# A chunk's output products grouped by form with the inverse's and the state's products, and low-rank second passes over all 128 weight rows

## The chip, the cores and the metric

The kernel runs on one core of a Trainium2 chip. The metric is the device time of one execution in microseconds (us). Three timed runs of the kernel before took 1186.85, 1188.13 and 1191.43 us; the median is 1188.13. One further execution was recorded by the hardware profiler.

The engines are named as in the profile: PE is the matmul engine, PEld its weight loads, DVE the vector engine, ACT the scalar engine, POOL the general one, SP the engine that issues most DMAs.

## What is computed

One layer of a hybrid block on 512 tokens of width 1024: an RMS norm, one wide input projection, three token mixers side by side (a gated short convolution, a gated linear recurrence, an RWKV-7 time mixing), a gated sum, an output projection, and an MLP with a squared ReLU. The part at issue is the RWKV-7 recurrence with 16 heads of 64 channels. Token by token the reference has:

```python
def step(state, inp):
    r_t, w_t, k_t, v_t, kk_t, a_t = inp
    sa = jnp.einsum('bhvk,bhk->bhv', state, -kk_t)
    state = (state * w_t[:, :, None, :]
             + sa[..., None] * (kk_t * a_t)[:, :, None, :]
             + v_t[..., None] * k_t[:, :, None, :])
    y_t = jnp.einsum('bhvk,bhk->bhv', state, r_t)
    return state, y_t
```

The decay `w` and the factor `a` come from low-rank products, `tanh(xw) @ w2` and `xa @ a2`, whose inner dimension is 64.

## The kernel before, in words

Activations lie with channels on the 128 partitions and the 512 tokens along the free dimension. The big projections are computed in three passes of a rounded number and its remainder (`mm3`, L153 to L155): high weights by high data, high by low, low by high. Each pass is a 128x512 matmul with 128 weight rows and 128 weight columns. Weights stream from DRAM in halves of 128x512; ACT rounds each (L131, `whi`) and DVE takes the remainder (L94, `wlo`).

The 16 heads go through the recurrence in four groups of four. For each group there are:

- `krv`: keys, receptances, values and the low-rank products for the group. A low-rank product is two passes: L402 and L408 with the rounded weights over all 128 rows, L403 and L409 with the weights' remainder. The data tiles `lws` and `las` hold the rounded inputs on one half of the rows and their remainders on the other; the weights `swh` and `swl` hold the same 64 rows twice.
- `amat` and `inverse`: the matrices of each chunk of 64 tokens, and the inverse of its triangular part.
- `chain`: the walk over the eight chunks, which carries the state. Each chunk has, for the four heads e = 2h + jj:
  - L550, into `pu`: products of `AXt` (128 weight rows, 64 columns) with `sv`, which holds the state on its upper half and the values on its lower;
  - ACT copies the result to `u0` (L552, L553);
  - L558, into `pu`: the inverse `TT` (64 rows, 64 columns) by `u0`; DVE copies the result into `sv` (L559, L560);
  - L567, into `pS`: `BKT` (128 rows, 64 columns) by `sv`; DVE makes the next state of it (`Stm`, `St`), and DVE and ACT copy that into the next chunk's `sv` (L545, L546);
  - the output `py`: for each head first L582, `RT` (64 rows, 64 columns) by the state, then L584, `AXt` (128 rows, 64 columns) by `sv`, which adds to it. ACT copies `py` to `Y` (L586).
- `post`: the norm of the outputs and the gate.

These products are float32, and each is two records in the profile. A group's first chunk starts from zero and leaves L582 out; the last chunk leaves L567 out. `pu`, `pS` and `py` have one buffer each, a PSUM bank.

A critical generator (`amat`, `inverse`, `chain`, `post`) is woven with a filler that issues projections of the same or the next group (`weave`, `segments`): after every step of the critical part some steps of the filler are emitted, by shares that are given as numbers. The critical part has a higher priority. The framework's scheduler then orders the instructions of each engine by priority and by its own estimates of when operands are ready; each engine executes its own list in order. `pin` (L157) is an exception: a matmul passed to it with a true first argument keeps its place behind the matmuls that the program emitted before it.

Of the kernel before, what the change touches and what calls it, by code (L numbers as in the profile page):

```python
# [9 lines left out]
F32 = mybir.dt.float32  # L10
# [8 lines left out]
P = 128  # L19
# priorities of the weight stream, the prologue and the critical steps over what is emitted beside them  # L20
OFF, OFFS, OFFP = 160, 20, 30
CP, CPI, CPP = 150, 60, 30
# empty steps that leave the latency of an inverse, or of a norm, to the filler
NINV, NPOST = 16, 6
# steps of the fillers, and their shares by part of the critical path
N_AB, N_KRV = 28, 24
# [3 lines left out]
S = 512  # L30
# [3 lines left out]
NC = 8  # L34
L = 64
# [53 lines left out]
def block_kernel(ctx, tc, xt, win, par, mulr, sw, wout, w1, w2, fg, cst, eyes, out):  # L89
    nc = tc.nc  # L90
    v, ac, gp, pe, sy = nc.vector, nc.scalar, nc.gpsimd, nc.tensor, nc.sync
# [18 lines left out]

# [1 line left out]
    ident = cp.tile([P, P], F32, name="ident")  # L112
    bd = cp.tile([P, P], F32R, name="bd")
    mask = cp.tile([P, P], F32, name="mask")
    part = cp.tile([P, len(PAR), KT], F32, name="part")
# [5 lines left out]

# [1 line left out]
    def load_w(src):  # L123
# [33 lines left out]
    def pin(first, mm):  # L157
        # in the order of the program, behind the matmuls before it
        if first:
            tc.keep_in_program_order(mm)  # L160

    def rsqrt(x, y, t):
        # Newton's steps from a first guess on the exponent; within 2 ulp after the third
        ts2(y.bitcast(I32), x.bitcast(I32), -0.5, RSQ, MUL, ADD)
        for _ in range(3):
            tt(t, x, y, MUL)
            stt(t, t, -0.5, y, MUL, MUL)
            stt(y, t, 1.5, y, ADD, MUL)

    def rsqrt_rows(pool, o, ps, low, scale=1.0):  # L170
        # rows alike in each 32: tokens to partitions, the root there, and back
        w = pool.tile([P, S], F32, tag="rqw", name="rqw")
        q = pool.tile([P, 3, 16], F32, tag="rqq", name="rqq")
        v.transpose(w, ps)
        wv = w.rearrange("p (b j) -> p b j", j=32)[:, :, 0]
        if scale == 1.0:
            v.tensor_scalar(out=q[:, 0], in0=wv, scalar1=low, scalar2=None, op0=MAX)
        else:
            ts2(q[:, 0], wv, scale, low, MUL, ADD)
        rsqrt(q[:, 0], q[:, 1], q[:, 2])  # L180
        v.transpose(o, q[:, 1].unsqueeze(2).to_broadcast([P, 16, 32]))

    # =======================================================================
    # projections and the three branches
    # =======================================================================
    ht_ctx = ExitStack()
# [7 lines left out]
    pc = ps.enter_context(tc.tile_pool(name="pc", bufs=1, space=PSUM))  # L194
# [99 lines left out]

    # low-rank inputs, and the first key tile, on x before its norm's scale
    def unscaled(t, tag):
# [8 lines left out]

    # derived per-channel values
    # sigmoid(z) = (1 + tanh(z / 2)) / 2 throughout: tanh shares its table with exp
    for i, (n, c) in enumerate((("mu_k", -1.0), ("mu_r", -1.0), ("ka", -0.5), ("mu_v", -1.0))):
# [12 lines left out]
    lws = sp.tile([P, S], F32R, name="lws")  # L321
    las = sp.tile([P, S], F32R, name="las")
# [14 lines left out]

    # softplus of the recurrence's parameter
    apv = part[:, PI["ap"]]
# [32 lines left out]
    def krv(g, G_):  # L372
# [5 lines left out]
        for jj in range(2):  # L378
            j = 2 * g + jj
# [3 lines left out]
            else:  # L383
                ks = WP("ks")
                t = yield from proj(("k", j))
# [11 lines left out]
            t = yield from proj(("r", j))  # L397
            shift(t, pv("mu_r", j), dvp(OMR, j), rs)
            yield
            swh, swl = load_sw(pk, "swa", j, 0, 2)  # L400
            pw = pm.tile([P, S], F32, tag="pm", name="pw")
            pe.matmul(pw, swh[:, 0], lws, start=True, stop=False)  # L402
            pe.matmul(pw, swl[0:64, 0], lws[0:64], start=False, stop=True)  # L403
            sig = WP("a1")
# [3 lines left out]
            pe.matmul(pa, swh[:, 1], las, start=True, stop=False)  # L408
            pe.matmul(pa, swl[64:128, 1], las[64:128], start=False, stop=True)  # L409
            av = WP("a4")  # L410
# [18 lines left out]
            tt(G_.BK[:, jj, :, 1], c3(kp), c3(pinv), MUL)  # L429
            # by head: the two tiles' halves side by side  # L430
            if jj == 0:
# [16 lines left out]
    def amat(G_):  # L448
        # A^T = [b|k]^T [a|r], masked
        G_.AX = sp.tile([P, 4, NC, 2, L], F32, tag="AXt", name="AXt")  # L450
# [24 lines left out]
    def inverse(G_):  # L475
# [8 lines left out]
        gp.dma_start(xt.rearrange("l s t -> l (s t)"), eyes)  # L484
        # xt[l, s, t] = X[t, s];  X[t, :] += A[t, s] X[s, :], la[l, s, t] = A[t, s]
        yield
# [39 lines left out]
    def chain(G_, c_lo, c_hi):  # L526
# [4 lines left out]
        St = G_.St  # L531
        for c in range(c_lo, c_hi):
# [22 lines left out]
            for jj in range(2):  # L555
                for h in range(2):
                    e = 2 * h + jj
                    pe.matmul(pu[64 * h:64 * h + 64, 2 + jj], TT[:, e * 8 + c], u0[:, e], start=True, stop=True)  # L558
            v.tensor_copy(sv[0:64, 0:2], pu[0:64, 2:4])  # L559
            v.tensor_copy(sv[0:64, 2:4], pu[64:128, 2:4])  # L560
            yield
            Sn = None
            if c < NC - 1:
# [9 lines left out]
                else:  # L573
                    tm = sp.tile([P, 2, L], F32, tag="Stm", name="Stm", bufs=2)
                    tt(tm, pS, St, ADD)
                    tt(Sn, tm, pl, MUL)
            py = pc.tile([P, S], F32, tag="py", name="py")[:, 0:2 * L].rearrange("p (j v) -> p j v", j=2)
            for jj in range(2):
                for h in range(2):
                    o = py[64 * h:64 * h + 64, jj]  # L580
                    if St is not None:
                        pe.matmul(o, RT[64 * h:64 * h + 64, jj, c], St[64 * h:64 * h + 64, jj],  # L582
                                  start=True, stop=False)
                    pe.matmul(o, AXt[:, 2 * h + jj, c, 1], sv[:, 2 * h + jj],  # L584
                              start=St is None, stop=True)
            ac.copy(G_.Y[:, c], py)  # L586
# [54 lines left out]
    def ab(q):  # L641
        # the recurrent branch, then the convolution's
        px = W("u2")
# [134 lines left out]
    for g in range(NG - 1):  # L778
        fl = fill_main(g)
        # steps of the two fillers, spread over 31 + 24 + 10 steps of the critical part  # L780
        nab = 2 * N_AB - (21 * R0 if g == 0 else 0)
        r2 = ((1 - P1) * nab + N_KRV) / (24 + 10 * WPOST)
        segments([(chainit(amat(GS[g]), inverse(GS[g])), P1 * nab / 31), (chain(GS[g], 0, NC), r2),
                  (post(g, GS[g]), WPOST * r2)], fl)
        drain(fl)

# [1 line left out]
    G_ = GS[NG - 1]  # L788
# [96 lines left out]

    # =======================================================================
    # MLP; the second norm's scale goes to its end
    # =======================================================================
    NA = 3 * NF // 4
    with tc.tile_pool(name="mw", bufs=2) as mw, \  # L890
# [34 lines left out]
        gp.memset(epst, EPS)  # L925
        # the square of the second norm's scale, by token
        sc2 = cp.tile([P, 4], F32, name="sc2")
# [127 lines left out]
```

## Time and profile before

| | us |
|---|---|
| timed runs, median of 3 (lowest, highest) | 1188.13 (1186.85, 1191.43) |
| profiled execution, span from first to last instruction | 1188.4 |
| PE busy | 1155.3 |
| DVE busy | 786.9 |
| ACT busy | 550.5 |
| the four walks over the chunks, first to last product | 55.2, 52.6, 52.6, 70.0 |

The profiler gives the profiled execution's span, with no time around it; it lies 0.3 us above the median of the timed runs. The walks are the stretches 180.5 to 235.7, 366.8 to 419.4, 550.6 to 603.2 and 716.6 to 786.6 us of the span. The last is longer because its filler and the norm of the first half of its tokens lie in it.

A row of the timeline has the start, the duration, the engine, the line, the operation, what it writes and reads, and the form. For PE the form is weight rows*weight columns, then rows x columns of the moving data. Matmuls overlap in the pipeline, so the cost of one on PE is read from start to start.

### The profile page before, as it was taken

What the parts mean: (1) busy time and instruction counts of PE and PEld (TensorE: products, weight loads), DVE (VectorE), ACT (ScalarE), POOL (GpSimd) and SP (SyncE); (2) the same over time, 40 slices, a digit from 0 to 9 for tenths busy, and PEclk for the clock granted to TensorE, in tenths of its full rate; (3) what the DMA queues carried; (4) which work ended last, traced back from release to release, by engine and by line L of the source; (5) the groups of instructions that cost most, each with busy time, mean ns of one, the idle gap of its engine ahead of it and who ended that gap; (6) DMA issues with size and microseconds to landing.
All of it is one profiled execution on the core that took longest, in us unless ns stands there. A gap on an engine that the chain in (4) does not pass through costs nothing.

```text
span 1188.4 us, 17270 instructions
## 1 busy us (share of the span) xinstructions
PE 1155.3 (97%) x6396; PEld 896.6 (75%) x6396; DVE 786.9 (66%) x1537; ACT 550.5 (46%) x1005; POOL 59.2 (5%) x99
## 2 busy tenths in 40 slices
PE   8999989999999999989999989999999999999996
PEld 4677876677777677767677766889888888888885
DVE  7997985689975678985688975677544444222225
ACT  6655364444556443565444545556444443222224
POOL 4100000000000000000000011000000000000003
PEclk9899988999999999999999999999999999999999
DMA  5231230222332122233122244436323333433322
GB/s 183 89 89 54 89 98 28 63 85 71 96 114 72 41 80 80 85 106 90 46 80 67 71 126 150 151 116 187 124 90 98 89 98 118 154 101 91 105 89 98
DMA packets 61973, 114.69 MB, mean 97 GB/s; under 512 B 7232, under 2 KB 10816, under 8 KB 61888
## 3 DMA queue, kind: packets, MB, share of 16 engines
q1 hardware_dynamic: 54960, 95.49, 26.2%
q0 software_dynamic: 6352, 17.30, 4.6%
q8 instruction: 50, 0.82, 0.3%
q10 hardware_dynamic: 576, 0.79, 0.2%
q14 instruction: 35, 0.29, 0.1%
HBM read 104.64 MB, written 8.91 MB: 96 GB/s over the span
## 4 chain that ended last, share of the span: by engine, by line
PE 84%; DVE 12%; issue 2%; ACT 1%; DMA 0%; SPq 0%; DVEq 0%; ACTq 0%
PE pp L153 12%; PE pp L155 11%; PE pp L154 11%; PE acc L153 6%; PE acc L154 6%; PE acc L155 6%; PE p L155 5%; PE p L153 5%; PE p L154 5%; DVE wlo L94 3%; PE py L582 2%; PE pA L458 2%; PE py L584 2%; DVE Z L94 2%; DVE dg L94 2%
## 5 line engine op out<-in xcount | busy, mean ns | idle before, releaser
L94 DVE TENSOR_TENSOR wlo<-raw,whi 128x512 fp32r<-128x512 f32 x340 | 235.4, 695 | 250.6 <-ACT whi L131 241.7
L131 ACT CAST whi<-raw 128x512 fp32r<-128x512 f32 x340 | 209.7, 619 | 379.1 <-PE acc L155 124.5
L155 PE MATMUL pp<-hh,wlo 128*128 128x512 f32 x696 | 284.4, 410 | 14.8 <-DVE wlo L94 14.5
L153 PE MATMUL pp<-hh,whi 128*128 128x512 f32 x696 | 285.0, 412 | 1.3 <-ACT hh L254 1.3
L154 PE MATMUL pp<-hl,whi 128*128 128x512 f32 x696 | 282.1, 407 | 3.1 <-DVE hl L97 3.1
L155 PEld LDWEIGHTS pp<-hh,wlo 128*128 128x128 f32 x696 | 133.2, 191 | 53.1 <-DVE wlo L94 21.6
L153 PEld LDWEIGHTS pp<-hh,whi 128*128 128x128 f32 x696 | 133.2, 191 | 34.6 <-issue 1.9
L154 PEld LDWEIGHTS pp<-hl,whi 128*128 128x128 f32 x696 | 133.4, 192 | 33.6 <-DVE hl L97 3.7
L155 PE MATMUL p<-h2h,wlo 128*128 128x512 f32 (+1 forms) x264 | 103.0, 390 | 0.1
L153 PE MATMUL p<-h2h,whi 128*128 128x512 f32 (+1 forms) x264 | 103.0, 390 | 0.0
L154 PE MATMUL p<-h2l,whi 128*128 128x512 f32 (+1 forms) x264 | 102.8, 389 | 0.0
L154 PE MATMUL acc<-wlo,ah 128*128 128x512 f32 x256 | 99.7, 390 | 0.0
L155 PE MATMUL acc<-whi,al 128*128 128x512 f32 x256 | 99.6, 389 | 0.0
L153 PE MATMUL acc<-whi,ah 128*128 128x512 f32 x256 | 99.6, 389 | 0.0
L155 PEld LDWEIGHTS p<-h2h,wlo 128*128 128x128 f32 x264 | 49.7, 188 | 11.6 <-DVE wlo L94 0.3
L154 PEld LDWEIGHTS p<-h2l,whi 128*128 128x128 f32 x264 | 49.7, 188 | 11.3
L153 PEld LDWEIGHTS p<-h2h,whi 128*128 128x128 f32 x264 | 49.7, 188 | 11.3
L154 PEld LDWEIGHTS acc<-wlo,ah 128*128 128x128 f32 x256 | 48.1, 188 | 10.1 <-DVE wlo L94 0.3
L153 PEld LDWEIGHTS acc<-whi,ah 128*128 128x128 f32 x256 | 48.1, 188 | 10.1
L155 PEld LDWEIGHTS acc<-whi,al 128*128 128x128 f32 x256 | 48.1, 188 | 10.0
L94 DVE TENSOR_TENSOR Z<-Z,dg 64x31 f32<-64x31 f32 (+15 forms) x124 | 42.2, 340 | 4.1
L94 DVE TENSOR_TENSOR dg<-Z 64x31 f32<-64x31 f32 (+15 forms) x124 | 42.2, 340 | 4.1
(299 smaller groups left out, 1591.3 us busy)
## 6 DMA issues: line engine op xcount, KB each, us to landing
raw<-in_win SPq DMA_DIRECT2D x180, 256.0 KB, 2.6
raw<-in_w SPq DMA_DIRECT2D x128, 256.0 KB, 2.7
raw<-in_wout SPq DMA_DIRECT2D x32, 256.0 KB, 2.6
swr<-in_sw SPq DMA_DIRECT2D x16, 128.0 KB, 2.1
x2T<-in_xt POOLq DMA_DIRECT2D x4, 512.0 KB, 7.1
x2d<-st POOLq DMA_DIRECT2D x8, 256.0 KB, 2.8
xr<-x2d POOLq DMA_DIRECT2D x1, 2048.0 KB, 8.7
xT<-in_xt SPq DMA_DIRECT2D x3, 512.0 KB, 6.8
```

The lines of the kernel that those rows point to most:

```text
L94: return v.tensor_tensor(out=o, in0=a, in1=b, op=op)
L131: ac.copy(hi, raw)
L153: pe.matmul(ps, wh, xh, start=start, stop=False)
L154: pe.matmul(ps, wh, xl, start=False, stop=False)
L155: pe.matmul(ps, wl, xh, start=False, stop=stop)
L458: pe.matmul(pts[h][:, ci], G_.BK[rows, jj, c], G_.AR[rows, jj, c], start=True, stop=True)
L582: pe.matmul(o, RT[64 * h:64 * h + 64, jj, c], St[64 * h:64 * h + 64, jj], start=True, stop=False)
L584: pe.matmul(o, AXt[:, 2 * h + jj, c, 1], sv[:, 2 * h + jj], start=St is None, stop=True)
```

## The change

It has two parts, and comments are dropped. In `chain`, `py` is taken from its pool before the second step's end, the four products of `RT` with the state (L582 before) are emitted right behind the four products of the inverse (L558), and the four of `AXt` with `sv` (L584 before) right behind the four of the state (L567 before). Both go through a new helper, `out_mm`, and so have one line, L564. The helper pins them: the `RT` products always, the `AXt` products behind the first always and the first too except in the last chunk. Only the first product of each half of the partitions clears the bank's flags (`start`). In `krv` the second low-rank passes take all 128 rows, which adds the product of the weights' remainder with the inputs' remainder.

```diff
-            pe.matmul(pw, swl[0:64, 0], lws[0:64], start=False, stop=True)
+            pe.matmul(pw, swl[:, 0], lws, start=False, stop=True)
...
-            pe.matmul(pa, swl[64:128, 1], las[64:128], start=False, stop=True)
+            pe.matmul(pa, swl[:, 1], las, start=False, stop=True)
...
                     pe.matmul(pu[64 * h:64 * h + 64, 2 + jj], TT[:, e * 8 + c], u0[:, e], start=True, stop=True)
+            py = pc.tile([P, S], F32, tag="py", name="py")[:, 0:2 * L].rearrange("p (j v) -> p j v", j=2)
+
+            def out_mm(w, x, h, jj, first, last, behind):
+                mm = pe.matmul(py[64 * h:64 * h + 64, jj], w, x, start=first and jj == 0, stop=last,
+                               skip_group_check=True)
+                pin(behind or h + jj > 0, mm)
+
+            if St is not None:
+                for jj in range(2):
+                    for h in range(2):
+                        out_mm(RT[64 * h:64 * h + 64, jj, c], St[64 * h:64 * h + 64, jj], h, jj, True, False, True)
             v.tensor_copy(sv[0:64, 0:2], pu[0:64, 2:4])
             v.tensor_copy(sv[0:64, 2:4], pu[64:128, 2:4])
             yield
...
-            py = pc.tile([P, S], F32, tag="py", name="py")[:, 0:2 * L].rearrange("p (j v) -> p j v", j=2)
             for jj in range(2):
                 for h in range(2):
-                    o = py[64 * h:64 * h + 64, jj]
-                    if St is not None:
-                        pe.matmul(o, RT[64 * h:64 * h + 64, jj, c], St[64 * h:64 * h + 64, jj],
-                                  start=True, stop=False)
-                    pe.matmul(o, AXt[:, 2 * h + jj, c, 1], sv[:, 2 * h + jj],
-                              start=St is None, stop=True)
+                    out_mm(AXt[:, 2 * h + jj, c, 1], sv[:, 2 * h + jj], h, jj, St is None, True, c < NC - 1)
             ac.copy(G_.Y[:, c], py)
```

PE's list in the second chunk of the second group, before, from the inverse's products to the next chunk's first ones (`pp` is a projection of the filler; sizes are those of what is written):

```order
L558 MATMUL pu<-u_3399,Z 64x64 x4
L153 MATMUL pp<-hh,whi 128x512
L154 MATMUL pp<-hl,whi 128x512
L155 MATMUL pp<-hh,wlo 128x512
L567 MATMUL pS<-sv,BKT 64x64 x4
L584 MATMUL py<-sv,AXt 64x64
L582 MATMUL py<-St,RT 64x64
L584 MATMUL py<-sv,AXt 64x64
L582 MATMUL py<-St,RT 64x64
L584 MATMUL py<-sv,AXt 64x64
L582 MATMUL py<-St,RT 64x64
L584 MATMUL py<-sv,AXt 64x64
```

Behind these come three `pp`, the fourth L582 (it is the next chunk's first) and the next L550. The same place in PE's list after the change:

```order
L558 MATMUL pu<-u_3399,Z 64x64 x4
L564 MATMUL py<-St,RT 64x64 x4
L154 MATMUL pp<-hl,whi 128x512
L580 MATMUL pS<-sv,BKT 64x64
L155 MATMUL pp<-hh,wlo 128x512
L580 MATMUL pS<-sv,BKT 64x64 x3
L564 MATMUL py<-sv,AXt 64x64 x4
L153 MATMUL pp<-hh,whi 128x512
L154 MATMUL pp<-hl,whi 128x512
L155 MATMUL pp<-hh,wlo 128x512
L153 MATMUL pp<-hh,whi 128x512
L550 MATMUL pu<-sv,AXt 64x64 x4
```

The four products of `RT` moved up behind the inverse's, those of `AXt` follow the state's without a break, and one `pp` parts the first state product from its three fellows. Over the program such a cut stands at 28 places.

DVE's list in the seventh chunk of the same group, before, from the copies of the inverse's products to the copy of the state into `sv` (`rqq`, `rs` and the tiles named a belong to the filler's `krv`):

```order
L559 COPY sv<-pu 64x128
L560 COPY sv<-pu 64x128
L97 SCALAR_TENSOR_TENSOR rqq<-rqq 128x16 x2
L94 TENSOR_TENSOR wlo<-raw,whi 128x512
L94 TENSOR_TENSOR Stm<-pS,St 128x128
L94 TENSOR_TENSOR rqq<-rqq 128x16
L97 SCALAR_TENSOR_TENSOR rs<-pp,part,rs 128x511
L94 TENSOR_TENSOR St<-Stm,pl 128x128
L97 SCALAR_TENSOR_TENSOR rqq<-rqq 128x16
L406 TENSOR_SCALAR a_3830<-a_3830 128x512
L545 COPY sv<-St 64x128
```

And after:

```order
L572 COPY sv<-pu 64x128
L573 COPY sv<-pu 64x128
L94 TENSOR_TENSOR rqq<-rqq 128x16
L97 SCALAR_TENSOR_TENSOR rs<-pp,part,rs 128x511
L94 TENSOR_TENSOR Stm<-pS,St 128x128
L97 SCALAR_TENSOR_TENSOR rqq<-rqq 128x16
L406 TENSOR_SCALAR a_3830<-a_3830 128x512
L94 TENSOR_TENSOR St<-Stm,pl 128x128
L97 SCALAR_TENSOR_TENSOR rqq<-rqq 128x16
L413 SCALAR_TENSOR_TENSOR a_3838<-smk,a_3830 128x512
L545 COPY sv<-St 64x128
```

The filler's scan over the tokens (L413) moved ahead of the state's copy, and a `wlo` moved ahead of the copies L572 and L573. On SP and POOL no transfer is added; two loads of small weights go out a few places earlier on SP.

## The prediction

> **What bounds the kernel now.** The page first: the span and the busy time of each engine, then the chain that ended last.
>
> ```profile
> span 1188.4 us, 17270 instructions
> PE 1155.3 (97%) x6396; PEld 896.6 (75%) x6396; DVE 786.9 (66%) x1537; ACT 550.5 (46%) x1005; POOL 59.2 (5%) x99
> PE 84%; DVE 12%; issue 2%; ACT 1%; DMA 0%; SPq 0%; DVEq 0%; ACTq 0%
> ```
>
> PE is busy nearly throughout and carries 84% of the chain. A mean says nothing of the stage that changes, so next come four stretches, from the first to the last product of each group's walk over its chunks (loop `chain`), in the view by windows. Each row has the stretch and its length, then the busy time of PE, PEld, DVE, ACT and POOL, then PE's granted clock, the DMA share and GB/s.
>
> ```profile
> 180.50:235.70 55.20, 55.20 (x406) 35.93 (x405) 34.36 (x94) 24.80 (x61) 1.59 (x3) 0.94 0.13 39
> 366.80:419.40 52.60, 52.60 (x407) 34.26 (x406) 34.25 (x94) 25.45 (x62) 1.59 (x3) 1.00 0.15 43
> 550.60:603.20 52.60, 52.60 (x407) 34.26 (x406) 34.24 (x94) 25.43 (x61) 1.59 (x3) 1.00 0.15 43
> 716.60:786.60 70.00, 69.74 (x531) 52.70 (x530) 41.98 (x103) 34.37 (x77) 3.90 (x7) 1.00 0.40 129
> ```
>
> In these 230.4 us PE has no idle time but 0.26 us, at a granted clock of 1.00 in three of them, while DVE is busy 65% and ACT 48% of the second stretch. So the stage is bound by PE's own sequence, and what PE saves there comes off the span until another engine is late. How PE spends it is read from its timeline, in the second group: the first chunk, then the second.
>
> ```profile
> 369.44 0.45 PE L567 MATMUL pS<-sv,BKT 128*64 128x64 f32 x8
> 369.72 0.40 PE L584 MATMUL py<-sv,AXt 128*64 128x64 f32 x8
> 370.05 0.50 PE L391 MATMUL pn<-bh,bd 128*128 128x512 f32 x1
> ...
> 372.88 0.45 PE L558 MATMUL pu<-u,Z 64*64 64x64 f32 x8
> 373.26 0.51 PE L153 MATMUL pp<-hh,whi 128*128 128x512 f32 x1
> 373.60 0.39 PE L154 MATMUL pp<-hl,whi 128*128 128x512 f32 x1
> 373.83 0.40 PE L155 MATMUL pp<-hh,wlo 128*128 128x512 f32 x1
> 374.16 0.45 PE L567 MATMUL pS<-sv,BKT 128*64 128x64 f32 x8
> 374.44 0.28 PE L584 MATMUL py<-sv,AXt 128*64 128x64 f32 x2
> 374.65 0.33 PE L582 MATMUL py<-St,RT 64*64 64x64 f32 x2
> 374.91 0.33 PE L584 MATMUL py<-sv,AXt 128*64 128x64 f32 x2
> ...
> 376.19 0.50 PE L153 MATMUL pp<-hh,whi 128*128 128x512 f32 x1
> ...
> 377.08 0.33 PE L582 MATMUL py<-St,RT 64*64 64x64 f32 x2
> 377.34 0.45 PE L550 MATMUL pu<-sv,AXt 128*64 128x64 f32 x8
> ```
>
> The first column is the start; the durations overlap, so prices are differences of starts. One product is two records (x2). Read the form, weight rows*columns, behind MATMUL. Wherever it changes from row to row, one product takes 0.26 us (374.65 to 374.91, 377.08 to 377.34). Where it stays, eight products take 369.44 to 370.05 = 0.61 us and four take 372.88 to 373.26 = 0.38 us, the step to the next form included: four more in one form cost 0.23 us. A 512-column matmul costs 373.83 - 373.60 = 0.23 us among its like, and 0.33 beside a change of form (373.83 to 374.16). The first chunk starts from zero and leaves L582 out, so before's own trace shows the eight products of one form that the change wants in every chunk.
>
> **The output products (L582, L584).** A chunk behind the first now takes 374.16 to 376.19 = 2.03 us for four state products, four of L584 and three of L582, and 377.08 to 377.34 = 0.26 for the L582 that the scheduler put ahead of the next chunk's work: 2.29 us. The new order puts the four L582 behind the four of the inverse (L558), which have the same 64*64 form, for 0.23 us, and the four L584 behind the four of the state, 0.61 us in all: 0.84 us. The difference is 1.45 us. A group's last chunk leaves L567 out, and 8 x 0.26 = 2.08 us become 0.38 + 0.23 = 0.61, which is 1.47, so one price does. There are 7 such chunks in each of 4 groups: 28 x 1.45 = **40.6 us**.
>
> Against that stand groups that the new order cuts. In 28 places a single product is parted from its seven or three fellows by one 512- or 256-column matmul. The cut-off one costs 0.26, and the seven that remain cost as much as eight, since products go in pairs (four for 0.38, two more for 0.115). The old order has about 7 such places: 21 x 0.26 = **5.5 us** back. How often PE goes from full-size matmuls to small ones and returns is 124 times in both, so those steps cancel. Left: 35.1 us.
>
> **The low-rank second passes (L403, L409)** have 64 weight rows before and 128 after, on the same 512 columns.
>
> ```profile
> 227.58 0.49 PE L403 MATMUL pw<-lws,swal 64*128 64x512 f32 x1
> 228.00 0.49 PE L408 MATMUL pa<-las,swah 128*128 128x512 f32 x1
> 228.42 0.49 PE L409 MATMUL pa<-las,swal 64*128 64x512 f32 x1
> 228.84 0.50 PE L153 MATMUL pp<-hh,whi 128*128 128x512 f32 x1
> ```
>
> Each step here is 0.42 us, where like follows like for 0.23. The 16 second passes alone give 16 x 0.19 = 3.0 us. With the neighbours that also pay for the change of form, a bare set of four takes 0.33 + 3 x 0.42 + 0.33 for the matmul behind it = 1.92 against 5 x 0.23 = 1.15, and 8 x 0.77 = 6.2 us is the most. Some stand beside small products and pay a change anyway; counted along the new order I get **5.0 us**. The extra rows cost nothing by these rows, as the 512 moving columns are unchanged. Gross: 35.1 + 5.0 = 40.1 us.
>
> **What becomes late.** PE needs DVE and ACT between its groups, and it reaches them sooner now.
>
> ```profile
> 373.45 0.28 DVE L559 COPY sv<-pu 64x128 f32<-64x128 f32 x1 [0.64 <-ACT whi L131]
> 373.76 0.29 DVE L560 COPY sv<-pu 64x128 f32<-64x128 f32 x1
> ...
> 375.01 0.29 DVE L94 TENSOR_TENSOR St<-Stm,pl 128x128 f32<-128x128 f32 x1
> ...
> 375.34 0.22 DVE L545 COPY sv<-St 64x128 f32<-64x128 f32 x1
> 376.30 0.27 ACT L586 COPY Y<-py 128x128 f32<-128x128 f32 x1 [2.92 <-PE py L584]
> ```
>
> From the inverse's products to the state's: the second copy ends at 374.05 and PE goes on at 374.16, 1.28 us after 372.88. The new order has eight products and mostly two or three matmuls there: 0.61 + 0.33 + 0.33 = 1.27 us with two, just enough. Where it has one (0.61 + 0.42 = 1.03), only one state product follows, which needs the first copy alone, at 373.73 + 0.11, or 0.96 us after. From the state's products to the next chunk's: St lands at 375.30, and the two copies into sv follow. ACT's waits behind the copy of Y, which now comes some 0.9 us after the state's first product and no longer 2.1, so sv is complete some 1.6 us after it. The shortest case in the new order has 0.61 + 0.33 + 2 x 0.23 + 0.33 = 1.73 us of PE work there, and most have nine matmuls. So a chunk fits while DVE is prompt. It won't always be: it holds 34.25 us of work in a stretch that shrinks from 52.6 to about 44, 78% of it. In the seventh chunk a scan now stands ahead of the copy L545.
>
> ```profile
> L413 DVE TENSOR_TENSOR_SCAN a<-smk,a 128x512 f32<-128x512 f32 x2 | 2.4, 1209 | 0.0
> L94 DVE TENSOR_TENSOR wlo<-raw,whi 128x512 fp32r<-128x512 f32 x7 | 4.8, 686 | 2.3 <-ACT whi L131 2.2
> ```
>
> These waits can't be read from before. Their lower end is nothing; their upper end is one 0.69 us operation of DVE in the way in every chunk, 28 x 0.7 = 20 us. I take 0.2 us a chunk, **6 us**, near the lower end, since slack and need agree to 0.1 us for a free DVE and only the scan's chunk shows a plain lateness (about 0.5). The other moved work is hidden: the loads of small weights go out a few places earlier on SP at a DMA share of 0.15. PE's new waits on itself ask for products at least twelve instructions back.
>
> Sum against the profiled span: 1188.4 - 40.1 + 6 = 1154.3 us. The median of the timed runs, 1188.13, is 0.3 us below that span. Forecast: **1154 us**.
>
> **Rivals.**
>
> 1. DVE sets the chunk's pace. For it: 78% load, in-order, long operations between the copies. Against: 0.2 us too little slack costs 0.2 us, not an operation. At 20 us of waits: 1188.4 - 40.1 + 20 = 1168 us.
> 2. The L582 products don't run in pairs when they stand side by side. No row shows two of them together: 0.23 us for four is the price of L558, whose two heads share weight rows, while L582's lie on rows 0 to 63 and 64 to 127. Unpaired, four cost 0.46: 28 x 0.23 = 6.4 us, so 1161. Alone each costs 0.26, so 1.04 is the upper end. The nearest products on alternating halves of the rows are these:
>
> ```profile
> 449.51 1.49 PE L458 MATMUL pA<-AR,BK 64*128 64x128 f32 x16
> 450.93 0.50 PE L155 MATMUL pp<-hh,wlo 128*128 128x512 f32 x1
> ```
>
> Eight take 1.42 us, 0.18 each with twice the columns, which fits pairs of 64-column products. The Trainium skill, "TensorEngine Tiling (Array Packing)", Restrictions and Gotchas, Gotcha 1, says that different row tiles cannot access one PSUM bank at the same time. The L582 of the two heads write one bank, so by that rule this rival holds; the rows above write two banks and don't test it.
>
> 3. Nothing but the alternation's look changes: products of one form on all rows don't overlap their weight loads, and the block stays at 2 us.
>
> ```profile
> L584 PEld LDWEIGHTS py<-sv,AXt x256: 132/136/227, 185.3 to 786.4; 128*64 128x64 f32 x128
> ```
>
> Sixteen loads one after another would take 16 x 0.136 = 2.2 us, as long as the block now, and only the low-rank 5 us would be left: 1183 us. Against it stands the 0.61 us of 369.44 to 370.05 for eight such products. The Trainium skill, "TensorE: Matmul & The Clock Gate", Part 3, The mechanism, says that a weight load overlaps matmuls in flight only when the row group differs; that would make this rival, and the 0.61 us speaks against it.
>
> 4. Slower. L582 now stands in PE's queue right behind L558, and its target py has one buffer, which ACT must have emptied (L586). If ACT is late, all of PE is held, the fillers too. The copy starts 0.11 us after py is done (376.30) and there are over 3 us until the next L582. It costs nothing until ACT is that far behind, and turns the sign at 40.1 / 28 = 1.43 us of holding a chunk more. With ACT at 48% I see no reason for it: 1.6 us of holding would give 1193 us.
>
> **Numbers.** Forecast with small waits (1149 to 1160 us) 0.62; no new waits at all, 1148 or just below, 0.05; DVE's pace 0.18; unpaired L582 0.10; no gain from the grouping 0.03; slower 0.02. The range runs from the sum without waits, less a microsecond that the last group's present waits could give, 1147, to 1168, where 0.2 us a chunk has become 0.7. About 0.5%, 6 us, is what a measurement of this kernel can tell from no change: faster by more than that 0.95, within it 0.03, slower 0.02.
>
> **What would show it.** In the profile after, eight products L558 and L564 should take 0.61 us, and eight of the state and L564 another 0.61, with no 0.26 us steps between them. L403 and L409 should be 128*128 at 0.23 us a step. The second and third stretch should shrink from 52.6 to about 44 us plus waits, PE's waits there should be on sv, on u and on little else, and the stages between the stretches should keep their lengths. A stretch that shrinks by less than 6 us, with PE waiting for DVE's copies, would be rival 1; 0.84 us for the L558 and L564 group would be rival 2.

## The result, and the profile after

| | before | after |
|---|---|---|
| timed runs, median (lowest, highest), us | 1187.49 (1185.57, 1191.43), 4 runs | 1150.67 (1145.85, 1151.48), 4 runs |
| span of the profiled execution, us | 1188.4 | 1148.5 |
| mean granted clock of PE in it | 0.985 | 0.988 |

By the medians the change takes off 36.8 us. The ratio of the times is 0.9673, with a 95% interval of 0.965 to 0.9697, which is 36.0 to 41.6 us. Two executions far above their fellows, one of 2679.6 us in the last experiment and one of 2167.68 us of the kernel before, are left out of the medians and ratios below. The profiled execution itself took 1150.27 us, so 1.8 us lie around its span; its span is 39.9 us shorter than the one of before. The forecast was 1154 us, the range 1147 to 1168.

The head of the page after, and the row on the chain of work that ended last:

```profile
span 1148.5 us, 17262 instructions
PE 1114.5 (97%) x6396; PEld 873.9 (76%) x6396; DVE 787.4 (69%) x1537; ACT 548.7 (48%) x1005; POOL 59.3 (5%) x99
...
PE 81%; DVE 13%; issue 3%; DMA 1%; ACT 1%; POOL 0%; SPq 0%; DVEq 0%; ACTq 0%; POOLq 0%
```

PE has as many records as before, 6396, and is busy 40.8 us less. PE still carries the chain, so the kernel is bound as it was. The four walks over the chunks, in the view by windows with the columns of before (stretch and length, then the busy time of PE, PEld, DVE, ACT, POOL, PE's granted clock, DMA share, GB/s):

```profile
178.80:224.80 46.00, 45.97 (x412) 31.34 (x411) 35.06 (x96) 25.03 (x61) 1.46 (x3) 0.93 0.14 46
354.70:399.20 44.50, 44.47 (x413) 30.17 (x412) 35.07 (x96) 25.94 (x62) 1.41 (x3) 1.00 0.15 48
527.80:572.30 44.50, 44.47 (x412) 30.15 (x411) 35.05 (x96) 25.96 (x62) 1.39 (x3) 1.00 0.17 49
684.90:746.10 61.20, 60.63 (x529) 46.81 (x528) 41.27 (x102) 33.58 (x77) 3.79 (x7) 1.00 0.43 141
```

They took 55.2, 52.6, 52.6 and 70.0 us before, so 34.2 us of the difference lie here. PE is busy in all of the second stretch but 0.03 us, and DVE 79% of it: as dense as the prediction had it, without waits of PE. The first three walks also hold five more 512-column matmuls of the filler than before (100 or 101 in place of 95 or 96, counted in the timeline), which at 0.23 us each is another 3.5 us of work that has left the stages between.

PE's timeline in the second chunk of the second group, the place that the prediction worked out:

```profile
361.00 0.38 PE L558 MATMUL pu<-u,Z 64*64 64x64 f32 x5
361.17 0.27 PE L564 MATMUL py<-St,RT 64*64 64x64 f32 x1
361.17 0.28 PE L558 MATMUL pu<-u,Z 64*64 64x64 f32 x3
361.28 0.40 PE L564 MATMUL py<-St,RT 64*64 64x64 f32 x7
361.60 0.49 PE L154 MATMUL pp<-hl,whi 128*128 128x512 f32 x1
362.03 0.33 PE L580 MATMUL pS<-sv,BKT 128*64 128x64 f32 x2
362.29 0.51 PE L155 MATMUL pp<-hh,wlo 128*128 128x512 f32 x1
362.72 0.39 PE L580 MATMUL pS<-sv,BKT 128*64 128x64 f32 x5
362.89 0.22 PE L564 MATMUL py<-sv,AXt 128*64 128x64 f32 x1
362.94 0.22 PE L580 MATMUL pS<-sv,BKT 128*64 128x64 f32 x1
362.95 0.45 PE L564 MATMUL py<-sv,AXt 128*64 128x64 f32 x7
363.33 0.50 PE L153 MATMUL pp<-hh,whi 128*128 128x512 f32 x1
```

Eight products of one form take 361.00 to 361.60 = 0.60 us, the four of `RT` among them; the seven that remain behind a cut take 362.72 to 363.33 = 0.61. The steps of 0.26 us are gone but one, the state product that a filler matmul cuts off (362.03 to 362.29). That matmul, with small products on both sides, takes 0.43 us to the next start (362.29 to 362.72).

The second low-rank passes have the form of their neighbours now, and L403 takes 389.93 - 389.70 = 0.23 us where only such matmuls stand around it (in the second walk):

```profile
389.70 0.39 PE L403 MATMUL pw<-lws,swal 128*128 128x512 f32 x1
389.93 0.40 PE L408 MATMUL pa<-las,swah 128*128 128x512 f32 x1
```

What PE waited for in the whole of the program, each row with the total, the number of times and the longest (us). Four rows of 0.2 to 0.9 us in total are left out; they are waits for `xgl`, `Y`, `v` and `bh`.

```profile
PE pp L155 <- DVE wlo L94: 14.5, 10, 3.4
PE pp L154 <- DVE hl L97: 3.1, 1, 3.1
PE pp L153 <- ACT xgh L228: 1.7, 1, 1.7
PE wu L220 <- POOL epst L217: 1.5, 1, 1.5
PE pp L153 <- ACT hh L254: 1.3, 1, 1.3
```

No row, shown or left out, has a product into `pu`, `pS` or `py`: nothing in the walks waits for `sv`, `u0` or an empty `py`. The 14.5 us for `wlo` and the 3.1 for `hl` stood in the profile before with the same numbers.

### The profile page after: what moved, and what is told of

Read it like the earlier page. It is cut to its first block, busy times and chain, and to the rows that moved or that the text cites. A ratio compares the mean times of both kernels' runs of the same rounds, so it can differ in the third digit from the quotient of the medians.

```text
span 1148.5 us, 17262 instructions
## 1 busy us (share of the span) xinstructions
PE 1114.5 (97%) x6396; PEld 873.9 (76%) x6396; DVE 787.4 (69%) x1537; ACT 548.7 (48%) x1005; POOL 59.3 (5%) x99
## 4 chain that ended last, share of the span: by engine, by line
PE 81%; DVE 13%; issue 3%; DMA 1%; ACT 1%; POOL 0%; SPq 0%; DVEq 0%; ACTq 0%; POOLq 0%
PE pp L155 12%; PE pp L154 11%; PE pp L153 11%; PE acc L154 6%; PE acc L153 6%; PE acc L155 6%; PE p L153 5%; PE p L155 5%; PE p L154 5%; DVE wlo L94 3%; PE pA L458 2%; DVE Z L94 2%; DVE dg L94 2%; DVE g L97 1%; PE py L564 1%
## 5 line engine op out<-in xcount | busy, mean ns | idle before, releaser
L155 PE MATMUL pp<-hh,wlo 128*128 128x512 f32 x696 | 285.8, 411 | 14.7 <-DVE wlo L94 14.5
L153 PE MATMUL pp<-hh,whi 128*128 128x512 f32 x696 | 282.0, 407 | 1.3 <-ACT hh L254 1.3
```

Source lines behind the costliest of these rows:

```text
L153: pe.matmul(ps, wh, xh, start=start, stop=False)
L155: pe.matmul(ps, wl, xh, start=False, stop=stop)
```

## The experiments

Three questions were left: what the two parts are worth alone, and whether it is the form or the order that counts; why the 6 us of waits did not come; and what the cuts cost, which the change left at 28 places.

### The parts alone

**The low-rank passes alone** (before, with these two lines):

```diff
-            pe.matmul(pw, swl[0:64, 0], lws[0:64], start=False, stop=True)
+            pe.matmul(pw, swl[:, 0], lws, start=False, stop=True)
-            pe.matmul(pa, swl[64:128, 1], las[64:128], start=False, stop=True)
+            pe.matmul(pa, swl[:, 1], las, start=False, stop=True)
```

> The kernel before with the low-rank second passes over all 128 rows alone; the output products stay as before. If a change of weight form is what costs (0.42 us a step where like follows like for 0.23), 5.0 us go: about 1182.5 us, with the walks of the second and third group some 1 us shorter each. If the grouping of the output products were all that matters, 1187.5 us.

Measured: 1182.94 us (10 runs) against 1188.14 (15 runs), ratio 0.9952 (0.9935 to 0.9968). That is 5.2 us by the medians, with 3.8 to 7.7 by the interval.

**The grouping alone** (the change, with the two lines above as they were before):

> The kernel after with the low-rank second passes over 64 rows as before; the output products grouped. Change of form: 36 us go (35.1 of the products, and a little where a low-rank pass now stands beside a small product): about 1151 us. If the two parts help each other or get in each other's way, the gains of this run and of the one with the low-rank passes alone would not add up to the 37 to 40 us of both.

Measured: 1151.80 us, ratio 0.9701 (0.968 to 0.9721): 36.3 us. The two parts add up to 41.5, where both together gave 36.8; each of the three is known to 2 to 3 us to either side. On top of the grouping the low-rank passes are thus worth 1.1 us by the medians (1151.80 and 1150.67), not 5.2. In the two traces the first walk ran at a granted clock of 0.93 with them (46.0 us) and at 1.00 without (44.0 us), while the second walk is 0.6 us shorter with them (44.5 and 45.1), so the clock may hide a part. How much was not tried.

### Form or order

**Before's order, one form.** `RT` is kept with zeros on the other head's rows, so that L582 takes 128 weight rows as L584 does; the two lines still alternate. (A scratch tile of the norm shares another's place, to make room.)

```diff
-        G_.RT = sp.tile([P, 2, NC, L], F32, tag="RT", name="RT")
-        ac.copy(G_.RT, G_.AR[:, :, :, 1])
+        if "RT" not in M:
+            M["RT"] = sp.tile([P, 2, 2, NC, L], F32, tag="RT", name="RT")
+            gp.memset(M["RT"], 0.0)
+        G_.RT = M["RT"]
+        for h in range(2):
+            ac.copy(G_.RT[64 * h:64 * h + 64, :, h], G_.AR[64 * h:64 * h + 64, :, :, 1])
...
-                        pe.matmul(o, RT[64 * h:64 * h + 64, jj, c], St[64 * h:64 * h + 64, jj],
+                        pe.matmul(o, RT[:, jj, h, c], St[:, jj],
```

> The kernel before with its old alternating order, but L582's weights padded with zeros to 128 rows (the other head's rows are zero, the state of both heads is the moving data), so all products of a chunk but the inverse's have one form, 128*64. If the change of form costs, the alternation in itself is free and the block of eleven products shrinks from 2.03 to about 0.8 us: 34 to 35 us go, 1153 us. If the alternation costs for another reason (each L584 adds to what L582 has just written and waits for it), the block stays at 2.0 us and the time at 1187 us. The padded weights need one more copy on ACT a group.

Measured: 1156.33 us, ratio 0.9732 (0.971 to 0.9754). PE's timeline at the block that took 2.03 us before (four products of the state, four of `AXt`, three of `RT`; the first rows and the last):

```profile
365.90 0.45 PE L572 MATMUL pS<-sv,BKT 128*64 128x64 f32 x8
366.18 0.22 PE L589 MATMUL py<-sv,AXt 128*64 128x64 f32 x1
366.19 0.22 PE L587 MATMUL py<-St,RT 128*64 128x64 f32 x1
...
366.54 0.28 PE L589 MATMUL py<-sv,AXt 128*64 128x64 f32 x2
366.75 0.50 PE L153 MATMUL pp<-hh,whi 128*128 128x512 f32 x1
```

The same eleven products in the same order take 366.75 - 365.90 = 0.85 us. So the alternation of operands costs next to nothing here; the change of the form from product to product cost the 1.18 us. This also settles the rival by which weight loads of one form don't overlap: `RT` has twice the weight rows, half of them zeros, and the block is less than half as long. The time falls by 31.8 us, 3 less than forecast; these 3 us were not followed.

**The `RT` products by themselves.** In the change, the four products of `RT` are emitted between the state's four and those of `AXt`:

```diff
-            if St is not None:
-                for jj in range(2):
-                    for h in range(2):
-                        out_mm(RT[64 * h:64 * h + 64, jj, c], St[64 * h:64 * h + 64, jj], h, jj, True, False, True)
             v.tensor_copy(sv[0:64, 0:2], pu[0:64, 2:4])
...
                     tt(Sn, tm, pl, MUL)
+            if St is not None:
+                for jj in range(2):
+                    for h in range(2):
+                        out_mm(RT[64 * h:64 * h + 64, jj, c], St[64 * h:64 * h + 64, jj], h, jj, True, False, True)
```

> The kernel after, but the four products of RT stand between those of the state and those of AXt instead of behind the inverse's: the alternation is gone, but two changes of form stay in each chunk. Change of form: three groups of four at 0.38 us, 1.14 us a chunk where the kernel after has 0.84, less some cuts that this order doesn't have: 4 us more than the kernel after, about 1155 us. If only the alternation cost, no more than the kernel after, 1150.7 us or a little below.

Measured: 1158.25 us (1154.82 to 1165.1), ratio 0.9757 (0.9727 to 0.9787): 7.6 us more than the change. The timeline at the same place:

```profile
362.28 0.45 PE L576 MATMUL pS<-sv,BKT 128*64 128x64 f32 x8
362.67 0.45 PE L564 MATMUL py<-St,RT 64*64 64x64 f32 x8
363.04 0.45 PE L564 MATMUL py<-sv,AXt 128*64 128x64 f32 x8
363.43 0.51 PE L154 MATMUL pp<-hl,whi 128*128 128x512 f32 x1
```

Twelve products in three forms take 1.15 us, 0.38 for each four; in the change eight of one form and four more of another's take 0.61 + 0.23 = 0.84. The 0.31 us are the price of two changes of form a chunk, 28 x 0.31 = 8.7 us at most. But the schedule moved as well: PE's list has 6 us of waiting for a tile of the inverse (`dg`) that the change's has not, 20 cut-off products in place of 28, and 160 of the filler's 512-column matmuls in the second walk in place of 101. How the 7.6 us divide stays open.

**Without the fixed order** (the change without `pin`):

```diff
-                pin(behind or h + jj > 0, mm)
```

> The change without the fixed order of the output products: the scheduler puts the four products of RT with the state apart from the inverse's in many chunks (three or one beside the first products of the next chunk, or alone among full-size matmuls). If the gain is the form's alone, the price is that of the added changes of form and cut-off products: 4 us over the change by step prices, 1155. If the order by itself does nothing and emitting the products in fours is enough: 1150 to 1151. If the fixed order costs something (waits), less than 1150.

Measured: 1156.93 us (1152.23 to 1157.56), ratio 0.9717 (0.9682 to 0.9753), whose interval overlaps the change's. The second walk is as long as the change's (44.30 us from first to last product, 44.27 there), the last one longer (64.35 and 60.94). The median lies 6.3 us above the change's, where step prices gave 4. The profiled execution is the shortest of the four (1152.23; the others 1156.71 and more), so these lengths need not be those of the others. A loss is likely and not shown.

### Why the waits did not come

**More work for DVE, for ACT.** In the change, a copy that nobody reads, `v.tensor_copy(junk, G_.v[0])` behind the copies into `sv`, or `ac.copy(junk, G_.v[0])` ahead of the copy of `py` to `Y`:

> The change with one more DVE copy of 128x512 in each of the 32 chunks, into a tile that nobody reads, right behind the two copies of the inverse's products into sv; it stands in DVE's list ahead of the state's update. If a chunk has the 0.1 us of slack that the prediction took, most of a copy of 0.3 to 0.7 us comes through in each of the 28 chunks that have a state update: 8 to 19 us over the 1150.7 of the change, 1159 to 1170. If DVE has room, as its 7 us a walk of waiting for PE in the trace after say (5.1 on the inverse's products, 2.0 on pS), most of the copy goes into that room: 0 to 5 us, 1151 to 1156.

> The change with one more ACT copy of 128x512 (0.6 us by other rows of ACT) in each of the 32 chunks, emitted ahead of the copy of py to Y, so that py is held longer. The slower rival (the state's output products stand in PE's queue and wait for py) would show waits of PE on py and 5 to 15 us more: 1156 to 1166. If there are over 2 us of room between the copy and the next products of RT, PE has no wait on py, and ACT at 58% of the walk still brings u0 and its half of sv nearly in time: 0 to 4 us more, 1151 to 1155.

Measured: 1151.24 us with DVE's copies, ratio 0.9675 (0.9634 to 0.9716); 1152.31 with ACT's, 0.9685 (0.9652 to 0.9719). Neither time answers the question. The second walk with DVE's copies, in the view by windows:

```profile
356.80:401.30 44.50, 44.48 (x412) 30.16 (x411) 34.95 (x96) 26.00 (x63) 1.30 (x3) 1.00 0.15 48
```

DVE is busy 34.95 us in the walk, as without them (35.07): the scheduler had put the copies outside, as they need nothing of the walk. By the starts in the two traces 28 of the 32 copies lie outside the walks, and four stand close together in the last one. Neither run loads every chunk of a walk, and neither tests the rivals. The next three read the walk's own products, so they stay in it.

**DVE later in each chunk.** Two copies out of `pu` ahead of those into `sv`; then four (`range(2)`):

```diff
+            junk = sp.tile([64, 2, L], F32, tag="junk", name="junk")
+            v.tensor_copy(junk, pu[0:64, 2:4])
+            v.tensor_copy(junk, pu[64:128, 2:4])
             v.tensor_copy(sv[0:64, 0:2], pu[0:64, 2:4])
             v.tensor_copy(sv[0:64, 2:4], pu[64:128, 2:4])
```

> The change with two more DVE copies of 64x128 out of pu into a tile that nobody reads, ahead of the two copies into sv in each of the 32 chunks. They read the inverse's products, so they can't be put outside the walks as the copies of the two runs before were: sv comes 0.57 us later in each chunk and DVE holds 4.6 us more a walk, 89% of 44.5 us. If a chunk has 0.1 us of slack, as the prediction reckoned from the order it had, 0.47 us comes through in each of 28 chunks: 13 us over the change, about 1164, with PE waiting for sv. If the filler's matmuls can be put between (PE's order puts two or three more of them there), the time stays: 0 to 3 us more, 1151 to 1154, and no wait of PE on sv.

> The same with four copies of 64x128 ahead: 1.15 us later a chunk and 9.2 us more of DVE a walk, which makes 44.3 of 44.5 us. The first rival, DVE's pace, must decide here: with DVE full, the walks grow by what DVE waits for PE in each of them (7 us in the second walk of the change, 20 to 28 us in all) or by part of it, 5 to 28 us over the change, 1156 to 1179, with waits of PE on sv or wlo. If the time still stays within 3 us of the change, DVE doesn't set the pace even then.

Beside them ran **the change again**:

> The change itself beside the three others on one chip, so that small differences are read against it: 1150.7 again, within 2 us.

Measured, against 1188.55 us before: the change 1151.19 (6 runs), ratio 0.9676 (0.9652 to 0.97); two copies 1150.87, 0.9682 (0.9659 to 0.9704); four copies 1181.49, 0.9939 (0.992 to 0.9958).

The copies by themselves are 0.57 and 1.15 us, but `sv` comes later than that. In the second chunk of the second group, its second copy in the change, then the inverse's products and the same copy with two copies more:

```profile
361.88 0.29 DVE L573 COPY sv<-pu 64x128 f32<-64x128 f32 x1
...
363.00 0.38 PE L558 MATMUL pu<-u,Z 64*64 64x64 f32 x5
364.58 0.29 DVE L576 COPY sv<-pu 64x128 f32<-64x128 f32 x1
```

From the first of the inverse's products to the end of that copy it is 362.17 - 361.00 = 1.17 us in the change and 364.87 - 363.00 = 1.87 here. Counted in the traces over all 32 chunks, the median is 1.17 us in the change, 2.37 with two copies and 4.15 with four, since DVE also runs work of the filler between the copies. So about 1.2 us more of delay a chunk costs nothing, and about 3.0 us costs 30 us. With two copies, the second walk and the stage behind it, in the view by windows:

```profile
356.00:408.10 52.10, 51.87 (x448) 36.32 (x447) 44.59 (x121) 29.97 (x69) 1.70 (x4) 1.00 0.19 58
408.10:528.00 119.90, 117.09 (x648) 92.34 (x644) 101.90 (x182) 61.97 (x103) 4.56 (x10) 1.00 0.31 95
```

And PE's only waits for `sv` in the whole program:

```profile
PE pS L583 <- DVE sv L575: 1.8, 1, 1.8
```

The second walk is 7.6 us longer, and holds 137 of the filler's 512-column matmuls in place of 101: 36 x 0.23 = 8.3 us. PE's time is not lost, it is spent on work that would have stood behind the walk, and the stage behind it is 119.9 us in place of 128.6. With four copies, the second walk, the stage behind it and the stage ahead of the last walk:

```profile
359.00:427.00 68.00, 67.60 (x508) 48.56 (x508) 56.35 (x148) 33.29 (x75) 1.70 (x4) 0.97 0.21 64
427.00:537.00 110.00, 105.10 (x584) 82.16 (x584) 95.29 (x172) 58.44 (x97) 4.56 (x10) 0.97 0.31 93
...
606.00:707.00 101.00, 90.52 (x528) 71.43 (x526) 81.57 (x151) 45.67 (x78) 8.87 (x17) 0.93 0.30 93
```

Two of PE's waits, the longest new one and that for `sv`:

```profile
PE pG L509 <- DVE dg L504: 9.5, 1, 9.5
...
PE pS L584 <- DVE sv L576: 1.1, 3, 0.4
```

Even here PE waits only 1.1 us for `sv`. The walk holds 196 filler matmuls and takes 68 us; the stage behind gives back 18.6 us (128.6 to 110.0) of the 23.5, and ahead of the last walk PE stands idle 10.5 of 101 us (4.8 of 112.6 in the change). Over the span PE is idle 1180.4 - 1128.2 = 52.2 us (1148.5 - 1114.5 = 34.0 in the change), 18 of the 32 us by which the spans differ; the other 14 are longer busy time, at a mean clock of 0.966. By the same windows 5.7 of the 18 us lie ahead of the last walk, 3.2 in it and 5.0 behind it. So the bill for a late DVE comes late in the program. That it comes there because the filler has run out is a reading of these rows, and was not tried.

**`py` held longer.** Three copies of `py` by ACT ahead of that to `Y`:

```diff
+            junk = sp.tile([P, 2, L], F32, tag="junk", name="junk")
+            for _ in range(3):
+                ac.copy(junk, py)
             ac.copy(G_.Y[:, c], py)
```

> The change with three more ACT copies of py (128x128, 0.27 us each) into a tile that nobody reads, ahead of the copy to Y in each of the 32 chunks: py is held 0.8 us longer, and ACT's next work is as much later. The slower rival would show waits of PE on py: if there is no room, 28 x 0.8 = 22 us over the change, 1173. If the next products of RT come over 2 us behind the copy, as the trace after has them, PE never waits for py: 0 to 3 us more, 1151 to 1154.

Measured: 1151.55 us, ratio 0.9685 (0.9662 to 0.9708), and no wait of PE on `py`. ACT's busy time rose by 18.7 us (567.4 and 548.7), 0.58 a chunk, all of it hidden. `py` is held longer than that, since ACT has other work between the copies. In the second chunk of the second group, and the next product of `RT`:

```profile
364.06 0.56 ACT L595 COPY junk<-py 128x128 f32<-128x128 f32 x2 [2.10 <-PE py L564]
365.00 0.26 ACT L596 COPY Y<-py 128x128 f32<-128x128 f32 x1
...
366.46 0.27 PE L564 MATMUL py<-St,RT 64*64 64x64 f32 x1
```

The copy to `Y` ends at 365.26, 1.29 us after `py`'s last product (363.97), and 1.20 us are left. Counted in the traces over all 32 chunks, the median from `py`'s last product to the end of that copy is 1.91 us, and 0.31 in the change: 1.6 us of holding more. The next product into `py` starts 0.76 us or more behind the copy, where the change has 2.09 or more.

### What a cut costs

The state product that is cut off is the first (`h` = 0): it needs DVE's first copy into `sv` alone, so the scheduler puts it ahead, while its fellows with `h` = 1 need the second. With the loops turned round the first product needs the later copy, and nothing is ready early:

```diff
-                pin(behind or h + jj > 0, mm)
+                pin(behind or (h, jj) != (1, 0), mm)
...
-                    for h in range(2):
+                    for h in (1, 0):
...
-                for h in range(2):
+                for h in (1, 0):
```

> The change with the second head half first in the state's and the chunk output's products, so that the first of them already needs DVE's second copy and the scheduler doesn't part one state product from its three fellows: 5 cuts in place of 28. If a cut costs what the trace after shows (0.26 us for the lone product and 0.2 more for the 512-column matmul beside it, 0.45 us), 23 fewer cuts give 10 us less than the change: 1140. If what stands in the cut only covers the wait for the second copy, and that wait appears in its place, 1148 to 1153.

Measured: 1141.60 us (5 runs), ratio 0.9588 (0.9557 to 0.962), below the change's interval: this version is faster than the change, by 9.1 us against its first median and 9.6 against its second. PE's timeline in the second chunk of the second group:

```profile
355.39 0.38 PE L558 MATMUL pu<-u,Z 64*64 64x64 f32 x5
...
356.65 0.45 PE L580 MATMUL pS<-sv,BKT 128*64 128x64 f32 x8
356.93 0.40 PE L564 MATMUL py<-sv,AXt 128*64 128x64 f32 x8
357.26 0.50 PE L155 MATMUL pp<-hh,wlo 128*128 128x512 f32 x1
```

The state's four products start 356.65 - 355.39 = 1.26 us after the inverse's, in one piece, and the block of eight takes 0.61 us. In this trace 5 cuts stand where the change has 28. 23 cuts fewer for 9.1 to 9.6 us is 0.39 to 0.42 us a cut, near the 0.45 that the trace of the change gave. The prediction's 0.26 a cut doesn't contradict this: there the number of steps between full-size matmuls and small ones was the same in both kernels, 124, as the two traces have it, and here it falls by 23.

## Why the prediction was right, and where it was off

- **PE's own sequence bounds the walks:** right. PE stayed without a gap there, and what its products saved came off the span.
- **The form sets the price:** right, and shown twice: 0.60 us for eight products and 0.61 for seven behind a cut in the change, and 0.85 us for eleven alternating ones once their form is the same.
- **Output products, 40.6 less 5.5 for the cuts:** 35.1 forecast, 36.3 measured alone.
- **Low-rank, 5.0 us:** 5.2 measured alone, with the bounds 3.0 and 6.2 around it; on top of the grouping only 1.1 by the medians, which stays open.
- **Waits, 6 us:** this is the term that was off. No wait of PE on `sv`, `u0` or `py` appears. The sum without it, 1148.3, is 0.2 us from the span of 1148.5. Part of this closeness is luck: by the medians the change is worth 36.8 or 37.4 us and not 40.1. Most of the 3 us between is the choice of the execution. Every execution with both numbers on record takes 1.7 to 1.9 us more than its span, so by this estimate the profiled one of before, with a span of 1188.4, took about 1190.2 us, 2.7 above the median. The 0.3 us that the forecast took off compared two executions. Luck also put the time, 1150.67, between 1149 and 1160, the outcome with small waits at a chance of 0.62, while the mechanism was that of no new waits, at 0.05: the 6 us of waits that did not come were half made up by these 3 us. The step that failed was "slack and need agree to 0.1 us": it read the slack off the order that PE had, as if that order were given. The order is the scheduler's answer to when `sv` will be ready. With `sv` later by about 1.2 us a chunk it puts other matmuls ahead, and the time stays.
- **DVE's pace (rival 1, 1168 us):** did not come; the runs with two and four copies show where it would decide, between about 1.2 and 3.0 us of a later `sv` a chunk, and that it would be paid for the most part late in the program.
- **Unpaired `RT` products (rival 2):** refuted, 0.60 us for eight where 0.84 was named. These products of two row tiles write one bank and cost no more than those that go in pairs. The Trainium skill, "TensorEngine Tiling (Array Packing)", Restrictions and Gotchas, Gotcha 1, says that they can't access it at the same time; here the measurement decides against a cost of it.
- **No gain from grouping (rival 3):** refuted by the 0.60 us, and by the padded `RT`.
- **Slower through `py` (rival 4):** refuted. With `py` held 1.6 us longer (median), past the turning point of 1.43 us that was named, PE never waited for it and the time stayed: the room of 2.09 us or more behind the copy took it.
- **Other stages keep their lengths:** nearly. From the first walk's end to the second's start it is 129.9 us, then 128.6, and 112.6, each about 1 to 3 us less than before; 3.5 us of that is the filler that moved into the walks, and the 1.3 us between the first two is the clock (below).

## What to carry over

Price small float32 matmuls by changes of form along PE's list, not by count: here a block of like form was cheap whatever its operands, and padding weight rows with zeros to keep the form was cheaper than the smaller product. Where a scheduler fills PE, a wait reckoned on one order is not a forecast of the next: ask how much filler is left, and for which stage. Look at which operand lets one product of a group go early; turning a loop so that the first needs the latest operand kept the groups whole here, for 9 us more. And measure in the trace how late an operand has become: copies of 0.57 us made it 1.2 us late, as other work stood between them.

## What the runs showed of the hardware

After like idle times PE's clock fell in one place and not in another, in one execution. In the change's trace, the windows behind the 2.7 us wait for `wlo` in the first and in the second stage between walks, in the view by windows:

```profile
319.20:321.80 2.60, 2.60 (x8) 2.02 (x7) 2.56 (x5) 0.00 (x0) 0.00 (x0) 0.54 0.33 101
...
493.30:496.00 2.70, 2.70 (x12) 2.17 (x12) 2.70 (x4) 0.00 (x0) 0.00 (x0) 1.00 0.27 97
```

PE's timeline at the two places:

```profile
318.66 0.79 PE L155 MATMUL pp<-hh,wlo 128*128 128x512 f32 x1 [2.68 <-DVE wlo L94]
319.25 0.63 PE L153 MATMUL pp<-hh,whi 128*128 128x512 f32 x1
...
493.10 0.50 PE L155 MATMUL pp<-hh,wlo 128*128 128x512 f32 x1 [2.69 <-DVE wlo L94]
493.43 0.40 PE L153 MATMUL pp<-hh,whi 128*128 128x512 f32 x1
```

After 2.68 us the first step is 0.59 us (318.66 to 319.25), and 2.6 us run at a clock of 0.54; after 2.69 us it is 0.33, at 1.00. The two stages differ by 1.3 us for it. The Trainium skill, "TensorE: Matmul & The Clock Gate", Part 1, ties the gate to a free-running activity window of about 3.4 us, and has the clock fall after an idle window. The trace agrees in that waits of one length did both, as where a window happens to lie would make it; but 2.68 us, less than a window, were enough, and here the measurement decides. The first walk also ran at 0.93 in the change's trace and at 1.00 in that of the turned loops (178.0 to 220.6 us). Executions of the change lie up to 8 us apart (the change again: 1145.1 to 1153.38). That the clock makes this spread was not tried: the mean clock was 0.994 in the shortest of them and 0.988 in the longest, but 0.984 in one of 1151.58 us.
